# An encoder block on one core: x handed in with channels on partitions, values projected in chunks of the depth

## The chip, the core and the metric

The kernel runs on one core of a Trainium2 chip. The metric is the device time of one execution in microseconds. Six engines take part: TensorE (PE; its weight loads are PEld), VectorE (DVE), ScalarE (ACT), GpSimd (POOL), and SyncE (SP), which issues most of the transfers; ScalarE and GpSimd have DMA queues of their own.

## The reference

One layer of a hybrid encoder, over two requests of 512 and 256 tokens (768 rows of 2048 channels, float32) with shared weights:

```python
h = rmsnorm(x, ln_mix_g)
z = h @ w_in                                  # 2048 x 2560: fourier 1024 | q 1024 | k 256 | v 256
of = fourier_mix(zf, w_fourier)               # Re(2-D DFT over positions and group channels), then a map per group
oa = window_attention(rope(q), rope(k), v, sink)   # 16 q heads, 4 kv heads of 64, window +-128
mixed = concat([rmsnorm(of, g_f), rmsnorm(oa, g_a)])
x = x + mixed @ w_out
u = relu(rmsnorm(x, ln_mlp_g) @ w_up)         # 2048 -> 8192
x = x + (u * u) @ w_down
y = rmsnorm(x, ln_final_g)
```

`rmsnorm` divides each row by the root of its mean square (plus 1e-6) and multiplies the channels by a gain.

## The kernel before

Every matrix product is made of three passes of a rounded 32-bit format: each operand is split into a high part (a rounding copy on ScalarE) and a low part (what is left, a subtraction on VectorE), and high x high, high x low and low x high are summed in PSUM. The function `split` (L66) does this.

The stages follow each other on TensorE. In the first, rows of x (`xt`, six blocks of 128) are transposed on TensorE (`four`, L435), multiplied by the gains of the channels while they leave PSUM (`evacuate`, L443) into `xr`, split into `xs` or into spare places, and multiplied with the 256 value columns of w_in (`v_proj`, L378), one row block after the other. ScalarE squares each row block as a whole (`row_norm`, L374); the factor `r0` per row is put on the values when they are split, and on all partitions as `rb` by a small matmul (`row_scale`, L398). Two of the split parts are also stored to DRAM as b11h and b11l (L508).

The second stage, `product7` (L256), forms the 1024 Fourier columns from 28 products of 24 passes: a scheme with seven products in place of eight over halves of the depth and of the tokens. Around product n the loop at the end of the second `with` block forms sums of weights (`sum7`), the high part of the weights for product n + 3 (`high7`, ScalarE), the low part for n + 2 (`low7`, VectorE), the operands of later products (`xsum`, `xhigh`, `xlow`), issues the loads for n + 5 (`load7`, on SP) and takes finished products out (`out7`). Near the end b11h and b11l are read back (`first_block`, L322).

The third stage projects q and k (the loop with `piece_load` and `piece_split`, L765 and L773) while the Fourier transform of the groups runs beside it; `fold(g)` there multiplies by `rb`. Its weights' columns are permuted while they are split. Attention and the output projection follow (`trans`, L900, turns the probabilities into th and tl), then the MLP.

In the first two stages the order on SP, ScalarE and VectorE is the order of the program text; a queue or an engine that waits holds everything that stands behind the waiting instruction.

## Time and profile before

| | us |
|---|---|
| median of 3 runs | 2588.84 (2587.99 to 2588.94) |
| span of the profiled execution | 2587.1 |
| TensorE busy | 2575.2 (100%) |
| VectorE busy | 1814.0 (70%) |
| ScalarE busy | 1124.0 (43%) |
| GpSimd busy | 250.6 (10%) |

The profiled execution took 2587.1 us from its first to its last instruction; the timed runs stand 1.7 us above that. By line, two lines of the MLP (L1195 and L1630) have 71% of the chain that ended last, the first three stages together about a tenth. The sections of the profile used below are the waits of TensorE, the chain of waits, the timeline, groups of instructions by line and shape, windows of time and the DMA issues.

### The profile page before, as it was taken

The page shows a single profiled execution, that of the slowest core. Times are in us where ns is not written, and L with a number is a line of the kernel's source. Part 1 is how long each engine was busy: PE and PEld are TensorE (multiplying, and loading weights), DVE is VectorE, ACT ScalarE, POOL GpSimd, SP SyncE. Part 2 cuts the span into 40 slices and gives each one's busy share as a digit, 9 for nine tenths or more (in the row PEclk, how much of TensorE's full clock was granted, in tenths as well). Part 3 has the DMA queues.
Part 4 walks back from the last instruction along what each step waited for, and adds up shares of the span by engine and source line. Part 5 has one row for each costly group of instructions (what it writes and reads, how often), then busy time and mean ns, then how long its engine had stood idle before and what let it go on. Part 6 is the DMA issues. An engine that isn't in the chain of part 4 may idle for free.

```text
span 2587.1 us, 35019 instructions
## 1 busy us (share of the span) xinstructions
PE 2575.2 (100%) x13580; PEld 2359.9 (91%) x13580; DVE 1814.0 (70%) x2222; ACT 1124.0 (43%) x1574; POOL 250.6 (10%) x353
## 2 busy tenths in 40 slices
PE   9999999999999999999999999999999999999998
PEld 9999998888899999999999999988888888888887
DVE  7966568776555656555877877667776765777687
ACT  6545437674333333333444544433333333333335
POOL 1001422222201011000000000110000000000000
PEclk9999999999999999999999999999999999999999
DMA  7863467555664445456666666675543662555364
GB/s 258 311 221 112 135 222 220 147 151 194 222 193 159 163 160 188 159 190 236 214 215 232 231 212 208 247 303 176 185 154 110 219 232 82 179 179 165 98 207 155
DMA packets 281879, 494.27 MB, mean 191 GB/s; under 512 B 20288, under 2 KB 177008, under 8 KB 280432
## 3 DMA queue, kind: packets, MB, share of 16 engines
q1 hardware_dynamic: 210208, 325.98, 39.7%
q10 hardware_dynamic: 58688, 115.18, 11.8%
q0 software_dynamic: 12816, 50.87, 5.8%
q8 instruction: 107, 1.75, 0.3%
q14 instruction: 60, 0.49, 0.1%
HBM read 365.07 MB, written 126.88 MB: 190 GB/s over the span
## 4 chain that ended last, share of the span: by engine, by line
PE 96%; DVE 1%; DMA 1%; issue 1%; ACT 0%; POOL 0%; SPq 0%; POOLq 0%; DVEq 0%; ACTq 0%
PE pu L1195 36%; PE pd L1630 35%; PE pm L1048 10%; PE p L268 4%; PE pz L804 4%; PE pv L391 1%; PE o L926 1%; PE s L850 1%; PE t L907 1%; DMA ofr<-ofd 0%; PE ptx L137 0%; PE pe L631 0%; DMA zf<-zf 0%; PE pa L610 0%; PE pt L137 0%
## 5 line engine op out<-in xcount | busy, mean ns | idle before, releaser
L1195 PE MATMUL pu<-xf,wh 128*128 128x384 f32 x3072 | 781.0, 335 | 0.0
L1195 PEld LDWEIGHTS pu<-xf,wh 128*128 128x128 f32 x3072 | 554.2, 188 | 1.5 <-ACT o L1213 1.2
L1630 PE MATMUL pd<-wh,sh 128*128 128x512 f32 x1332 | 518.5, 389 | 0.0
L1630 PE MATMUL pd<-wl,sh 128*128 128x512 f32 x1332 | 518.4, 389 | 0.0
L1630 PE MATMUL pd<-wh,sl 128*128 128x512 f32 x1332 | 518.2, 389 | 0.0
L1195 PE MATMUL pu<-xf,wl 128*128 128x384 f32 x1536 | 513.9, 335 | 0.0
L1607 ACT ACTIVATE wh<-rd 128x1024 fp32r<-128x1024 f32 x200 | 202.4, 1054 | 521.9 <-PE pd L1630 422.2
L1617 DVE TENSOR_TENSOR wl<-rd,wh 128x1024 fp32r<-128x1024 f32 x200 | 236.2, 1221 | 225.8 <-ACT wh L1607 225.1
L1175 ACT ACTIVATE wh<-ur 128x1024 fp32r<-128x1024 f32 x160 | 170.0, 1063 | 382.7 <-PE pu L1195 211.3
L1630 PEld LDWEIGHTS pd<-wl,sh 128*128 128x128 f32 x1332 | 250.2, 188 | 51.7
L1630 PEld LDWEIGHTS pd<-wh,sl 128*128 128x128 f32 x1332 | 250.2, 188 | 51.7 <-DVE sl L1618 0.3
L1630 PEld LDWEIGHTS pd<-wh,sh 128*128 128x128 f32 x1332 | 250.2, 188 | 51.5
L1195 PEld LDWEIGHTS pu<-xf,wl 128*128 128x128 f32 x1536 | 288.5, 188 | 0.0
L1181 DVE TENSOR_TENSOR wl<-ur,wh 128x1024 fp32r<-128x1024 f32 x160 | 195.6, 1222 | 76.0 <-ACT wh L1175 76.0
L1216 DVE TENSOR_TENSOR o<-pu,o 128x768 f32<-128x768 f32 x160 | 152.9, 956 | 122.5 <-PE pu L1195 115.0
L1600 DVE TENSOR_TENSOR rd<-rd 128x1024 f32<-128x1024 f32 x112 | 131.8, 1218 | 0.0
L1195 PE MATMUL pu<-xs,wh 128*128 128x384 f32 x512 | 130.0, 334 | 0.0
L1175 ACT ACTIVATE wh<-sx 128x1024 fp32r<-128x1024 f32 x64 | 67.8, 1062 | 130.3 <-PE pu L1195 101.9
L268 PE MATMUL p<-xs,wh 128*128 128x384 f32 x448 | 114.0, 335 | 0.0
L1618 DVE TENSOR_TENSOR sl<-sr,sh 128x768 fp32r<-128x768 f32 x111 | 105.6, 951 | 0.0
L1181 DVE TENSOR_TENSOR wl<-sx,wh 128x1024 fp32r<-128x1024 f32 x64 | 78.2, 1223 | 23.8 <-ACT wh L1175 23.6
L1195 PEld LDWEIGHTS pu<-xs,wh 128*128 128x128 f32 x512 | 92.5, 188 | 0.0
(277 smaller groups left out, 3903.1 us busy)
## 6 DMA issues: line engine op xcount, KB each, us to landing
rd<-in_w_down SPq DMA_DIRECT2D x176, 512.0 KB, 5.1
ur<-in_w_up SPq DMA_DIRECT2D x128, 512.0 KB, 3.9
sr<-sd SPq DMA_DIRECT2D x95, 384.0 KB, 5.3
pd<-o ACTq DMA_DIRECT2D x60, 384.0 KB, 2.3
o<-pd POOLq DMA_DIRECT2D x60, 384.0 KB, 6.1
sd<-sm ACTq DMA_DIRECT2D x60, 384.0 KB, 2.9
raw<-in_w_in SPq DMA_DIRECT2D x38, 512.0 KB, 4.9
raw<-in_w_out SPq DMA_DIRECT2D x32, 512.0 KB, 4.9
```

The lines of the kernel that those rows point to most:

```text
L268: nc.tensor.matmul(ps7[bank, g, r][:, :HALF], l[:, i, r * P : (r + 1) * P], x[:, o, 4 * e + i, :], start=(opens and e == 0 and i == 0 and ...
L804: nc.tensor.matmul(ps[c][s][:, :HALF], w[:, i, cs], whole[j // 2][s][o][:, 4 * (j % 2) + i, :], start=first and n == 0, stop=stop and n == 2,)
L1048: nc.tensor.matmul(ps, l(k), w[:, k % 2, :], start=(k == 0 and n == 0), stop=(k == 7 and n == 2))
L1175: nc.scalar.activation(wh[:], raw[:], AF.Copy)
L1181: nc.vector.tensor_tensor(out=wl[:], in0=raw[:], in1=f32(wh[:]), op=ALU.subtract)
L1195: nc.tensor.matmul(ps[:, t, :HALF], w[:, i, t * P : (t + 1) * P], xb[:, o, i, :], start=(s == first_of[bank] and i == 0 and n == 0), stop= ...
L1216: nc.vector.tensor_tensor(out=o, in0=src, in1=o, op=ALU.add)
L1600: add = lambda x, y, op: nc.vector.tensor_tensor(out=x[:], in0=x[:], in1=y[:], op=op)
L1607: nc.scalar.activation(wh[:], t[:], AF.Copy)
L1617: nc.vector.tensor_tensor(out=wl[:], in0=t[:], in1=f32(wh[:]), op=ALU.subtract)
L1618: nc.vector.tensor_tensor(out=sl[:], in0=sr[:], in1=f32(sh[:]), op=ALU.subtract)
L1630: nc.tensor.matmul(o, l[:, q, ts], w[:, ns], start=(j == j0 and (q, t) == (0, 0)), stop=(j == j1 and (q, t) == (1, 2)),)
```

## The change

The host now hands x in a second time with channels on partitions (`x_t`), the three gains side by side, and w_in in blocks of 256 columns whose rows of one partition lie together; the q and k columns come in the order in which they are used. The values of all six row blocks are summed side by side in six PSUM banks, over nine chunks of the depth. The rows of x are loaded for their squares alone, during products 11 to 23, and the row factor `r0` is no longer put on the values but on the transposed probabilities in the attention; `rb` is made by a store to DRAM and a load to all partitions. The core of the diff (the functions that go away are in the listing above):

```diff
-    w_in = a["w_in"].rearrange("(k p) c -> p k c", p=P)
+    w_in = a["w_in"]
...
+    ssq = stat("ssq", NM * 4)
+    r0_d = dpool.tile([1, T], F32, tag="r0d", name="r0d")
...
-                    nc.sync.dma_start(raw[:], w_in[:, k0 : k0 + 4, c0 : c0 + 256])
+                    nc.sync.dma_start(raw[:], w_in[c0 // 256][:, k0 : k0 + 4, :])
...
+            flat = xs[1][:].rearrange("p o k t -> p (o k t)").rearrange("p (s o t) -> p s o t", s=8, o=2)
+            vt = xp.tile([P, 4, 2, HALF], F32R, tag="vt", name="vt")
+            room = [flat[:, 0:4], flat[:, 4:8], vt[:]]
+            chunks = [(0, 1), (1, 1), (2, 2), (4, 2), (6, 2), (8, 2), (10, 2), (12, 2), (14, 2)]
+            homes = [(0, 0), (0, 1), (0, 2), (1, 0), (1, 2), (2, 0), (0, 0), (1, 0), (2, 0)]
...
+            def load_x(k0, n):
+                for t in range(2):
+                    nc.sync.dma_start(xr[k0 // 8][t][:, k0 % 8 : k0 % 8 + n, :], a["x_t"][:, t, k0 : k0 + n, :])
+
+            def load_wv(k0, n, queue=nc.sync):
+                queue.dma_start(wv[k0 // 4][:, k0 % 4 : k0 % 4 + n, :], w_in[9][:, k0 : k0 + n, :])
+
+            def prepare(c):
...
+                for i in range(n):
+                    nc.scalar.activation(raw[0][:, i], raw[0][:, i], AF.Copy, scale=g0[:, k0 + i : k0 + i + 1])
+                gb = g0[:, k0 : k0 + n].rearrange("p (k o) -> p k o", o=1).to_broadcast([P, n, HALF])
+                nc.vector.tensor_tensor(out=raw[1], in0=raw[1], in1=gb, op=ALU.mult)
+                split(wh, wl, wv[w][:, wk, :])
+                for t in range(2):
+                    split(*parts[t], raw[t])
...
+            def v_term(c, m, term, i):
+                k0, n = chunks[c]
+                l, r = ((0, 0), (0, 1), (1, 0))[term]
+                k = k0 + i
+                nc.tensor.matmul(
+                    pv[m][:, :256], xhl[c][m // 3][l][:, i, m % 3 * P : (m % 3 + 1) * P], whl[k // 4][r][:, k % 4, :],
+                    start=(k == 0 and term == 0), stop=(k == NK - 1 and term == 2),
+                )
+
+            def v_keep(m):
+                split(vhl[:, m, :, 0, :], vhl[:, m, :, 1, :], pv[m][:, :256].rearrange("p (g d) -> p g d", g=NKV))
...
+            for i in range(15):
+                nc.tensor.matmul(pw[:, :P], ones[:], ones[:], start=True, stop=True)
+            nc.scalar.activation(mhalf[:, 7:8], mhalf[:, 7:8], AF.Copy)
+            nc.scalar.dma_start(gall[:], a["gains"])
+            load_wv(0, 1, nc.scalar)
+            load_x(*chunks[0])
+            load_wv(1, 1, nc.scalar)
+            load_x(*chunks[1])
...
+            for c, (k0, n) in enumerate(chunks):
+                prepare(c)
+                if c == 5:
+                    for o in range(2):
+                        nc.scalar.dma_start(b11_d[o][:], f32(xs[0][:, o]))
+                    nc.scalar.dma_start(ident[:], a["c_ident"])
+                if c + 1 < len(chunks):
+                    for term in range(3):
+                        for m in range(NM):
+                            for i in range(n):
+                                v_term(c, m, term, i)
                 else:
...
+                    for n2 in range(2):
+                        high7(n2)
+                        low7(n2)
+                    for m in range(NM):
+                        for term in range(3):
+                            for i in range(n):
+                                v_term(c, m, term, i)
+            for n in range(2):
+                xsum(b11, b12, b11, n)
+            for m in range(NM):
+                v_keep(m)
+
+        def row_load(i):
+            m, h = divmod(i, 4)
+            xt = raw7["x", i] = hq["p"].tile([P, 512], F32, tag="xt", name="xt", bufs=3)
+            nc.sync.dma_start(xt[:], x_rows(m)[:, h * 512 : (h + 1) * 512])
+
+        def row_square(i):
+            xt = raw7.pop(("x", i))
+            nc.scalar.activation(xt[:], xt[:], AF.Square, accum_out=ssq[:, i : i + 1])
+
+        def row_norms():
+            nc.vector.tensor_reduce(out=ss0[:], in_=ssq[:].rearrange("p (m h) -> p m h", h=4), op=ALU.add, axis=AX.X)
+            rsqrt_of(r0[:], ss0[:], D, NM, nc.gpsimd)
+            nc.gpsimd.dma_start(r0_d[0].rearrange("(m p) -> p m", p=P), r0[:])
+            nc.gpsimd.dma_start(rb[:], r0_d[0].partition_broadcast(P))
...
                 load7(n + 5)
+                for i in range(2 * n - 22, 2 * n - 20):
+                    if 0 <= i < 4 * NM:
+                        row_load(i)
+                    if 1 <= i <= 4 * NM:
+                        row_square(i - 1)
+                if n == 24:
+                    row_norms()
...
-                wh, wl = in_w[p] = [wpool.tile([P, 4, 256], F32R, tag=f"w{c}", name=f"w{c}", bufs=4) for c in "hl"]
-                hi, lo = (w[:].rearrange("p i (d h) -> p i h d", h=4) for w in (wh, wl))
-                split(hi, lo, raw[:].rearrange("p i (h d) -> p i h d", h=4))
+                in_w[p] = wsplit(raw)
...
-        later(t_th, lambda: nc.scalar.activation(th[:], pt[:], AF.Copy))
-        later(t_tl, lambda: nc.vector.tensor_tensor(out=tl[:], in0=pt[:], in1=f32(th[:]), op=ALU.subtract))
+        rk = r0[:, k0 + kb : k0 + kb + 1]
+        later(t_th, lambda: nc.scalar.activation(th[:], pt[:], AF.Copy, scale=rk))
+        later(t_tl, lambda: nc.vector.scalar_tensor_tensor(
+            out=tl[:], in0=pt[:], scalar=rk, in1=f32(th[:]), op0=ALU.mult, op1=ALU.subtract
+        ))
...
+    x = np.concatenate([given["x_prompt"], given["x_sample"]], 0)
+    given["x_t"] = x.T.reshape(NK, P, 2, HALF).transpose(1, 2, 0, 3)
+    given["gains"] = np.concatenate([given.pop(n) for n in _GAINS]).reshape(3 * NK, P).T
+    w = given["w_in"].reshape(NK, P, IN_W // 256, 256).transpose(2, 1, 0, 3)
+    turned = w[4:9].reshape(5, P, NK, 4, HD).swapaxes(3, 4).reshape(5, P, NK, 256)
+    given["w_in"] = np.concatenate([w[:4], turned, w[9:]], 0)
```

Three places of the order. First TensorE at the start. Before (pw are warm-up passes, pt and pg transposes, pv values; xs_290 and xs_291 hold the low or high parts of x's two halves):

```order
L474 MATMUL pw<-ones 128x128 x7
L137 MATMUL pt<-ident,xt_307 128x128 x4
L423 MATMUL pg<-ident,gt 128x16
L137 MATMUL pt<-ident,xt_307 128x128 x12
L474 MATMUL pw<-ones 128x128 x6
L391 MATMUL pv<-wh,xs_290 128x256 x16
L391 MATMUL pv<-wh,xs_291 128x256 x16
L137 MATMUL pt<-ident,xt_316 128x128 x8
L391 MATMUL pv<-wl,xs_290 128x256 x8
L137 MATMUL pt<-ident,xt_316 128x128 x8
L391 MATMUL pv<-wl,xs_291 128x256 x8
```

After:

```order
L417 MATMUL pw<-ones 128x128 x15
L407 MATMUL pv<-wh,xs_292 128x256 x3
L407 MATMUL pv<-wh,xs_293 128x256 x3
L407 MATMUL pv<-wl,xs_292 128x256 x3
L407 MATMUL pv<-wl,xs_293 128x256 x3
L407 MATMUL pv<-wh,xs_292 128x256 x3
L407 MATMUL pv<-wh,xs_293 128x256 x3
L407 MATMUL pv<-wh,xs_292 128x256 x3
L407 MATMUL pv<-wh,xs_293 128x256 x3
```

The transposes are gone from between the value passes, and each group of value passes now belongs to one slice of the depth and three row blocks.

Second, ScalarE in the same stage, around the two stores. Before:

```order
L462 ACTIVATE xs_291<-xr_287 128x512 x2
L462 ACTIVATE xs_291<-xr_289 128x512 x2
L72 ACTIVATE vhl<-pv,r_268 128x4x64
L375 ACTIVATE xt_531,ss_267<-xt_531 128x2048
L508 DMA b11h<-xs_290 128x3072
L508 DMA b11l<-xs_290 128x3072
L406 COPY rb<-pb 128x128
L462 ACTIVATE vt<-xr_287 128x512 x2
L462 ACTIVATE xs_291<-xr_289 128x512 x2
```

After, with what each waits for (DMAHW5 is the semaphore lane that the store b11h counts up; vt and xs_293 are places of split parts):

```order
L69 ACTIVATE wh<-raw 128x512 [waits DMAHW7_49]
L69 ACTIVATE vt<-xr_290 128x2x384 [waits Activation_49]
L69 ACTIVATE vt<-xr_291 128x2x384 [waits DVE_49]
L441 DMA b11h<-xs_292 128x3072
L441 DMA b11l<-xs_292 128x3072 [waits DMAHW2_49]
L442 DMA ident<-in_c_ident 128x128 [waits DMAHW5_49]
L394 ACTIVATE xr_290<-xr_290,gall 128x384 x2
L69 ACTIVATE wh<-raw 128x512
L69 ACTIVATE xs_293<-xr_290 128x2x384 [waits PE_49,Activation_49]
L69 ACTIVATE xs_293<-xr_291 128x2x384 [waits DVE_49,PE_49]
```

The identity load, which stood first of all before, now stands behind the stores with a wait for the lane of the first one, and the scaling and splitting of the next chunk stand behind it.

Third, SP near the end of `product7`. Before (wr are weights of a product, xf the parts read back, raw on L79 the weights of the next stage):

```order
L225 DMA wr<-in_w_in 128x4x256 x2
L79 DMA raw<-in_w_in 128x4x256
L225 DMA wr<-in_w_in 128x4x256
L326 DMA xf_1761<-b11h 128x3072
L79 DMA raw<-in_w_in 128x4x256
L326 DMA xf_1762<-b11l 128x3072
L225 DMA wr<-in_w_in 128x4x256
L79 DMA raw<-in_w_in 128x4x256 x4
```

After, with waits (xt are the row loads, of which each waits for a square on ScalarE):

```order
L227 DMA wr<-in_w_in 128x1024 [waits DMAHW1_49,DVE_49]
L79 DMA raw<-in_w_in 128x1024 [waits DMAHW5_49,DMAHW2_49,DVE_49]
L464 DMA xt<-in_x_sample 128x512 [waits DMAHW3_49,Activation_49]
L464 DMA xt<-in_x_sample 128x512 [waits DMAHW4_49,Activation_49]
L328 DMA xf_1647<-b11h 128x3072 [waits DMAHW5_49]
L328 DMA xf_1648<-b11l 128x3072 [waits DMAHW0_49,DVE_49]
L227 DMA wr<-in_w_in 128x1024 [waits DMAHW1_49]
L464 DMA xt<-in_x_sample 128x512 [waits DMAHW2_49,Activation_49]
L464 DMA xt<-in_x_sample 128x512 [waits DMAHW3_49,Activation_49]
L79 DMA raw<-in_w_in 128x1024 [waits DMAHW6_49,DMAHW2_49,DVE_49]
```

The last weight load of the stage now has row loads ahead of it as well as the two reads, and the last two row loads stand behind it.

## Rows read from the trace of the kernel before

**Rows 1.** Page, its head and part 1: busy us, share of the span, instructions.

```profile
span 2587.1 us, 35019 instructions
...
PE 2575.2 (100%) x13580; PEld 2359.9 (91%) x13580; DVE 1814.0 (70%) x2222; ACT 1124.0 (43%) x1574; POOL 250.6 (10%) x353
```

**Rows 2.** Waits of TensorE: total us, times, longest us.

```profile
PE pv L391 <- ACT wh L69: 1.1, 1, 1.1
...
PE pc L567 <- ACT of L633: 0.4, 1, 0.4
```

**Rows 3.** Chain of waits, 0 to 120 us: start us, us, what.

```profile
0.73 3.34 DMA ident<-in_c_ident
...
21.25 5.75 PE pv L391 x48
27.00 1.75 PE pt L137 x16
...
56.38 63.79 PE p L268 x368
```

**Rows 4.** Timeline of the start: start us, us, engine, line, instruction.

```profile
1.04 3.36 PE L474 MATMUL pw<-ones 128*128 128x128 f32 x14 [1.04 <-DVE mhalf L56]
...
1.65 1.28 ACT L462 ACT_TABLE_LOAD   x1 [1.65 <-PEq L1796]
...
7.96 1.50 PE L474 MATMUL pw<-ones 128*128 128x128 f32 x12
```

**Rows 5.** Groups of ScalarE, 0 to 57 us: busy us, mean ns, idle before.

```profile
L462 ACT ACTIVATE xs<-xr 128x512 fp32r<-128x512 f32 x20 | 12.2, 632 | 12.3 <-DVE xr L452 12.0 <-ACT xs L462 0.3
...
L69 ACT ACTIVATE wh<-raw 128x1024 fp32r<-128x1024 f32 x4 | 4.1, 1052 | 0.4 <-DMA raw<-in_w_in 0.3
L72 ACT ACTIVATE vhl<-pv,r 128x256 fp32r<-128x256 f32 x7 | 3.2, 462 | 1.9 <-PE pv L391 1.9
```

**Rows 6.** Timeline of VectorE, two low parts of product weights.

```profile
91.58 1.22 DVE L253 TENSOR_TENSOR wl<-wr,wh 128x1024 fp32r<-128x1024 f32 x1
...
140.54 1.23 DVE L253 TENSOR_TENSOR wl<-wr,wh 128x1024 fp32r<-128x1024 f32 x1 [0.44 <-ACT wh L245]
```

**Rows 7.** Windows of 1 us: busy us by engine, PEclk, DMA share, GB/s.

```profile
1.00:2.00 1.00, 0.96 (x4) 0.96 (x5) 0.00 (x1) 0.35 (x1) 0.00 (x0) 1.00 0.14 23
8.00:9.00 1.00, 1.00 (x12) 1.00 (x11) 1.00 (x3) 0.69 (x2) 0.00 (x0) 1.00 1.07 378
43.00:44.00 1.00, 1.00 (x12) 1.00 (x10) 1.00 (x2) 0.04 (x1) 0.74 (x2) 1.00 1.12 479
```

**Rows 8.** Timeline of ScalarE and its queue around the first store.

```profile
40.26 0.36 ACTq L508 DMA_DIRECT2D b11h<-xs  x1
...
40.69 0.45 ACT L72 ACTIVATE vhl<-pv,r 128x256 fp32r<-128x256 f32 x1
```

**Rows 9.** DMA issues, 56 to 176 us: count, KB each, median us to landing.

```profile
wr<-in_w_in SPq DMA_DIRECT2D x18, 512.0 KB, 6.8
...
xf<-b11h SPq DMA_DIRECT2D x1, 1536.0 KB, 9.2
```

**Rows 10.** Groups of ScalarE, 330 to 700 us.

```profile
L910 ACT ACTIVATE th<-t 128x512 fp32r<-128x512 f32 x56 | 32.7, 594 | 10.5 <-PE t L907 3.2 <-PE s L850 1.9 <-DVE tl L911 1.6
...
L1080 ACT ACTIVATE xc<-pm,r 128x512 f32<-128x512 f32 x24 | 16.3, 681 | 2.0 <-PE pm L1048 1.7
...
L1386 ACT ACTIVATE pm<-yp 128x512 f32<-128x512 f32 x14 | 8.4, 597 | 7.5 <-DVE yp L1380 7.3
...
L1386 ACT ACTIVATION_READ_ACCUMULATOR pm<-yp 128x1 f32 x14 | 2.6, 186 | 0.0
```

**Rows 11.** Window 104 to 152 us.

```profile
104.00:152.00 48.00, 48.00 (x279) 48.00 (x278) 39.88 (x34) 25.85 (x27) 0.00 (x0) 1.00 0.78 260
```

**Rows 12.** DMA issues, 0 to 60 us.

```profile
xt<-in_x_prompt SPq DMA_DIRECT2D x8, 256.0 KB, 5.9
```

**Rows 13.** Groups of ScalarE, 56 to 173 us.

```profile
L69 ACT ACTIVATE wh<-raw 128x1024 fp32r<-128x1024 f32 x4 | 8.2, 2051 | 6.3 <-PE p L268 3.8 <-DMA zf<-z 2.5
```

More of the change, by code (lines that the diff above doesn't have):

```diff
@@ new lines, in hybrid_encoder @@
+            whl = [[wpool.tile([P, 4, 256], F32R, tag=t, name=t, bufs=4) for t in ("wh", "wl")] for _ in range(4)]
+            flat = xs[1][:].rearrange("p o k t -> p (o k t)").rearrange("p (s o t) -> p s o t", s=8, o=2)
[3 more added lines that the diff above has]
+            homes = [(0, 0), (0, 1), (0, 2), (1, 0), (1, 2), (2, 0), (0, 0), (1, 0), (2, 0)]
@@ new lines, in hybrid_encoder @@
+            xhl = {}
+            def load_x(k0, n):
[5 more added lines that the diff above has]
+                k0, n = chunks[c]
+                r, s0 = homes[c]
+                ks = slice(k0 % 8, k0 % 8 + n)
+                raw = [xr[k0 // 8][t][:, ks, :] for t in range(2)]
+                rows = [room[r][:, s0 + i * n : s0 + i * n + n] for i in range(2 if k0 >= 8 else 1)]
+                if k0 < 8:
+                    parts = [[xs[0][:, o, ks, :] for o in range(2)]]
+                else:
+                    parts = []
+                parts += [[x[:, :, o, :] for o in range(2)] for x in rows]
+                xhl[c] = parts
+                w, wk = k0 // 4, slice(k0 % 4, k0 % 4 + n)
+                wh, wl = (x[:, wk, :] for x in whl[w])
+                for i in range(n):
[5 more added lines that the diff above has]
+                    split(*parts[t], raw[t])
@@ new lines, in hybrid_encoder @@
+            pv = [pp.tile([P, 512], F32, tag="f" if m < 4 else "ps", bufs=4, name="pv") for m in range(NM)]
+            def v_term(c, m, term, i):
+                k0, n = chunks[c]
+                l, r = ((0, 0), (0, 1), (1, 0))[term]
[4 more added lines that the diff above has]
+                )
@@ new lines, in hybrid_encoder @@
+            load_wv(1, 1, nc.scalar)
+            load_x(*chunks[1])
+            load_wv(2, 2)
+            load_x(*chunks[2])
+            load_wv(4, 4)
+            load_x(*chunks[3])
+            load_x(*chunks[4])
+            load_wv(8, 4)
+            load_x(*chunks[5])
+            load_x(*chunks[6])
+            load_wv(12, 4)
+            load_x(*chunks[7])
+            load_x(*chunks[8])
+            load7(0)
+            load7(1)
+            for c, (k0, n) in enumerate(chunks):
[9 more added lines that the diff above has]
+                                v_term(c, m, term, i)
+                else:
+                    for n2 in range(2):
[5 more added lines that the diff above has]
+                                v_term(c, m, term, i)
@@ L768, in piece_load @@
                 j, c0 = p % 4, cols[p // 4]
-                in_raw[p] = wload(w_in[:, 4 * j : 4 * j + 4, c0 : c0 + 256], 4, 256)
+                in_raw[p] = wload(w_in[c0 // 256][:, 4 * j : 4 * j + 4, :], 4, 256)
             elif p < n_in + 2:
```

146 lines of the change are left out of this document (9 added, 137 removed).

## Prediction

> **What bounds the kernel now.** I read the page first: TensorE is busy for 2575.2 of 2587.1 us [rows 1]. Its waits come next; the largest is 1.1, before the first value pass, and one of 0.4 in the z stage will matter below [rows 2]. So time can come only from work that TensorE no longer does or from an earlier start, and it can be lost to new gaps. The chain of waits of the first 120 us then says what TensorE does before `product7`: per block of 128 rows 48 value passes in 5.75 (0.12 each) and 16 transposes in 1.75, until the first product starts at 56.38; from there 368 passes follow without a gap, 0.1733 each, so a product (24 passes) is 4.16 [rows 3]. The run takes 2588.84 (median); the profiled one has a span of 2587.1. I leave the 1.7 around the span as it is and take the differences from 2588.84.
>
> **The start.** TensorE loses 96 transposes of x, the transposes of the gains and the row-scale passes. The 288 value passes stay, 288 x 0.12 = 34.6. They come in nine chunks of the depth, two of 18 passes (one slice) and seven of 36 (two slices, 36 x 0.12 = 4.32).
>
> When does the first one start? ScalarE begins with the table load (1.28 [rows 4]), from about 0.7 to 2.0, does a tiny activation until 2.2, issues the gains (0.44 for such an issue, an estimate from the issues beside it) and the first slice of w_v at 2.65. A small load, the identity, took 3.34 to land [rows 3]; so gains 5.5, w_v 6.0. Per slice ScalarE scales 384 columns, splits 256 and splits 384 twice. 256 columns took 0.46, 512 0.63, 1024 1.05 [rows 5]; I take 0.5 + 0.46 + 2 x 0.5 = 1.96 for one slice, 2 x 0.5 + 0.63 + 2 x 0.85 = 3.33 for two. The first pass has its operands at 5.5 + 0.5 + 0.46 + 0.5 = 7.0; ScalarE is through with chunk 0 at 7.5, with chunk 1 at 9.4, and has the first operand of chunk 2 at 9.4 + 1.0 + 0.63 + 0.85 = 11.9, the second 0.85 later, so TensorE gets into chunk 2 at about 12.2. From there TensorE's 4.32 a chunk is the longest: ScalarE needs 3.33, VectorE (a gain multiply and two low parts of 768 columns, one of 512, at 1.22 for 1024 [rows 6]) about 3.5. A chunk's transfers, 1.05 MB at the 378 GB/s seen while loads pile up [rows 7], take 2.8. Without a stall the values end at 12.2 + 7 x 4.32 = 42.4 and the first product starts 56.4 - 42.4 = **14.0 earlier**. The six splits of the values now lie together behind that point; product 0 has other PSUM banks, so they cost 0, and 6 x 0.46 = 2.8 if it had to wait for them all.
>
> **A new wait in that stage.** Behind chunk 5 ScalarE issues the stores b11h and b11l and then the identity load, which waits for b11h's completion; chunk 6's scaling is queued behind it. Before, b11h went out at 40.26 and the next activation ran at 40.69 [rows 8]: nothing was held. The issue is now at 9.4 + 4 x 3.33 = 22.8. The rate with both stores alone reached 479 GB/s [rows 7]; b11h's 1.57 MB at that are 3.3, with a little over 1 to start and end about 4.5. But SP still loads x and w_in then, and the same block on its way back took 9.2 among other loads [rows 9]. So the wait ends 4.5 to 11 after the issue (9.2 and a fifth more), at 27.3 to 33.8. Chunk 6 then needs 1.0 + 0.63 + 0.85 = 2.5 before its first pass, which TensorE wants at 12.2 + 4 x 4.32 = 29.5: a stall of 0.3 to 6.8. I take **3.1**, a landing of 7.3, between the ends, since SP's loads run out while the store is under way. The Trainium skill, DMA: Bandwidth & Descriptors, section Queues, rings and completion order, says that a DMA engine takes turns between the queues that have work for it, a packet at a time. By this rule b11h, with every second turn, would move for 6.6 instead of 3.3, land after 7.8, and the stall would be 3.6. No row of before has two loaded queues side by side long enough to test it, and the sum goes without it.
>
> **The row norms.** 24 loads of 256 KB and 24 squares (128x512 with an accumulator read) come into products 11 to 23. The nearest pair, L1386, is 0.60 + 0.19, overlapping by about 0.1 [rows 10]: 0.68, or 1.4 a product. ScalarE was busy 25.85 of 48 us there [rows 11], 2.2 a product; 3.6 of 4.16 fits. But ScalarE now also waits for loads, and the weights' high parts stand behind. There are three buffers and load i goes out when square i-3 is done, so two squares and two landings L must fit in three products: 2 (L + 0.75) < 12.5, L < 5.5. Loads of 512 KB landed here after a median of 6.8 [rows 9], those of 256 KB at the start after 5.9 [rows 12]. At 5.9 a product would take 4.43, 3.3 more over 12 products; at 6.8 it is 5.03, 10.4 more. The weights' low parts stood ready some 5 us ahead for product 10 (92.8, product at 98.0) and 10 for product 23 (141.8, product at 152.1) [rows 3, 6]; a mean cover of 7 takes that much off. Bounds 0 and 10.4; I take **+3.4** (6.8 with the cover), the more so as the last two squares stand in front of a weight's high part with two 1.5 MB reads before their loads on SP.
>
> **Smaller terms.** Columns turned beforehand take the 20 splits of the q/k weights from 2.05 [rows 13] to 1.05 [rows 5] on ScalarE, on VectorE alike. The 0.4 in the z stage goes [rows 2]: **-0.4**, with 0 as the other bound. In the attention 56 copies of 594 become like the 681 with a row scale [rows 10], 4.9 of ScalarE; VectorE's 56 subtractions become scaled ones, taken alike. TensorE's passes of L1048 hide both, since its list of waits has nothing of theirs [rows 2]: 0, and 9.8 if that cover were gone. The row scale goes to DRAM in 768 pieces of 4 bytes and back to all partitions; from product 24 there are four products, 16.6, for two landings: 0 while each is under 8, and 3 if one takes 11.
>
> **Sum:** 2588.84 - 14.0 + 3.1 + 3.4 - 0.4 = 2580.9, that is 7.9 faster; its own range is 2577.5 to 2584.5.
>
> **Rivals.** (a) Both stalls are hidden: the store lands in 4.5 and the row loads keep under 5.5. 2588.8 - 14.0 + 0.3 - 0.4 = 2574.7. For it: the cover of 5 to 10. Against: SP's traffic at both places.
> (b) The gain is eaten: the store takes 11 (+6.8), and L is 6.8 with only the cover of 5 (+5.4): -14.0 + 6.8 + 5.4 - 0.4 = -2.2, 2586.6, no change. For it: the 9.2 and the median of 6.8.
> (c) Slower: the row loads and the weights' loads starve each other. In 104 to 152 the queues moved 260 GB/s at a share of 0.78 [rows 11]; 6.3 MB more in 50 us is 126 GB/s, in all 386, as much as was moved while loads piled up [rows 7]. If L goes to 8.6, a product takes (8.6 + 0.75) x 2/3 = 6.23, 24.9 more over 12, 17.9 after a cover of 7: -14.0 + 3.1 + 17.9 - 0.4 = +6.6, 2595.4. It decides from L = 7.8 (5.7 a product), where nothing of the gain is left. Against it: w_in now comes in 4 KB runs instead of 1 KB, and the loads may shift by the cover.
> (d) TensorE starts on its low clock. The granted clock reads 1.00 (2.4 GHz) from the first microsecond [rows 7], but the first 14 warm-up passes took 0.24 each and 12 later ones 0.125 [rows 4], which is 1.2 against 2.4 GHz. Now 15 passes end at 4.6 and TensorE rests until 7.0, where before it went on with transposes. If the first 36 value passes took 0.24, they would end at 15.6, 3.4 late: 2584.3. The Trainium skill, TensorE: Matmul & The Clock Gate, Part 1, holds that the low clock is the default, that activity releases it and that rest brings it back; by that the rest speaks for (d), and rows of before show only the rise.
>
> **How the numbers follow.** Forecast 0.43, (a) 0.16, (b) 0.19, (c) 0.14, (d) 0.08. Under 0.2% (5.2 us) a measurement can't tell this kernel from unchanged. Faster: (a), 0.39 of the forecast, half of (d), 0.59. Slower: (c), 0.14. Within 0.2%: the rest, 0.27. To hold the time 8 times in 10 the range goes from (a) past (b), half way to (c): 2574.5 to 2591.
>
> **What would show it.** The first product starts at 45 to 46, with one gap of TensorE of about 3 before chunk 6 and ScalarE idle until the identity load goes out: the first two terms are right; without that gap, (a). Gaps of 3 to 4 in all between products 17 and 27, ended by a high or low part of a weight: the third. If from product 14 on most products take over 5 and ScalarE's idle ends with row loads, (c). Value passes of 0.24 at the start, (d). A new gap after 175 us would prove wrong what I cost at nothing there.

## The result, and the profile after

The changed kernel takes 2594.49 us (median of 9 runs, 2593.0 to 2597.2) beside 2588.88 for the kernel before on the same chip (9 runs): a ratio of 1.0024, 95% interval 1.0014 to 1.0033. It is 5.6 slower. The forecast was 2580.9 and the range ended at 2591.0; both missed.

The page's head and part 1 of the changed kernel, which answer to [rows 1]: TensorE works 4.3 less than before, and yet the span is 5.4 longer.

```profile
span 2592.5 us, 34872 instructions
...
PE 2570.9 (99%) x13474; PEld 2351.7 (91%) x13474; DVE 1791.3 (69%) x2204; ACT 1116.8 (43%) x1619; POOL 241.9 (9%) x339
```

The waits of TensorE over the whole of it (total us, times, longest), where [rows 2] had 1.1 and 0.4:

```profile
PE p L270 <- ACT wh L247: 4.3, 1, 4.3
PE pv L407 <- ACT xs L69: 4.1, 2, 3.6
PE p L270 <- DVE z L287: 1.2, 1, 1.2
...
PE p L270 <- DVE wl L255: 0.9, 2, 0.7
...
PE p L270 <- ACT z L290: 0.3, 1, 0.3
```

Two waits of about 4 are new: one in the values (L407), one in `product7` (L270). To see in which stage the time went I took the start of each stage's first TensorE pass from the timeline (the products on L270, the q and k projection, the scores, the up and the down projection) and subtracted, in one profiled execution of each kernel:

| | first product at | product stage | q/k stage | scores to first up pass | up | first down pass to the end of the last |
|---|---|---|---|---|---|---|
| before | 56.1 | 116.6 | 205.2 | 352.8 | 933.8 | 914.5 |
| after | 47.9 | 128.0 | 204.3 | 354.3 | 934.7 | 914.5 |

The start gave 8.2 instead of 14.0 less a stall of 3.1. The product stage took 11.4, that is these 8.2 and 3.2 more. Behind it the two differ by 1.5 in all up to TensorE's last pass, and by 0.7 in what follows that pass: 5.4 together, as in the spans.

**The start.** TensorE's timeline of the changed kernel (start us, us, engine, line, instruction, count, idle before):

```profile
1.04 6.33 PE L417 MATMUL pw<-ones 128*128 128x128 f32 x30 [1.04 <-DVE mhalf L56]
7.12 0.96 PE L407 MATMUL pv<-wh,xs 128*128 128x256 f32 x6
...
12.18 1.12 PE L407 MATMUL pv<-wh,xs 128*128 128x256 f32 x7 [0.49 <-ACT xs L69]
...
33.34 2.39 PE L407 MATMUL pv<-wh,xs 128*128 128x256 f32 x12 [3.62 <-ACT xs L69]
35.53 2.46 PE L407 MATMUL pv<-wl,xs 128*128 128x256 f32 x12
...
47.91 0.52 PE L270 MATMUL p<-xs,wh 128*128 128x384 f32 x2
```

The first value pass comes at 7.12 (forecast 7.0), chunk 2 at 12.18 (12.2); then TensorE rests 3.62 before chunk 6. The 15 warm-up matmuls are two passes each, 30 in all; the last of them starts at 7.09, so TensorE doesn't rest before the first value pass. ScalarE and its queue there, which answer to [rows 8]:

```profile
21.33 0.34 ACTq L441 DMA_DIRECT2D b11h<-xs  x1
...
30.54 0.34 ACTq L442 DMA_DIRECT2D ident<-in_c_ident  x1
30.92 1.12 ACT L394 ACTIVATE xr<-xr,gall 128x384 f32<-128x384 f32 x2 [8.76 <-DMA b11h<-xs]
```

The store landed after 9.19; the identity load waited for it, and chunk 6's scaling stood behind that load. After the rest comes something that the sum had no term for: the next 24 passes start 2.19 per 12 and then 2.30, against 1.44 per 12 elsewhere. Windows of the changed kernel (us, then busy us by engine, PEclk, DMA share, GB/s) show why:

```profile
34.00:38.00 4.00, 4.00 (x23) 4.00 (x22) 4.00 (x6) 4.00 (x9) 0.00 (x0) 0.57 0.59 233
...
164.00:170.00 6.00, 5.54 (x16) 5.03 (x17) 5.44 (x8) 3.80 (x6) 3.09 (x3) 0.50 0.46 165
```

The granted clock fell to its lower level (0.50 is 1.2 GHz) after each of the two long rests. The first cost about 1.6 (4.49 for 24 passes instead of 2.88), the second more: from 164.21 two products took 11.7 instead of 8.3.

**The product stage.** Of its 11.4, 6.7 are listed as TensorE's waits on L270. Taken from the starts of the passes, against the 0.1733 from one to the next in the kernel before, the whole can be placed: 4.4 in the long wait behind the pass at 159.6, 3.4 at the low clock behind it, and 3.7 in six short waits ahead of it (11.5; the stage before has 0.1 of such excess itself). The chain of waits there (start us, us, what):

```profile
151.28 11.13 DMA xt<-in_x_sample
...
163.46 0.71 ACT wh L247
```

SP's timeline says why these row loads were late and what stood behind others:

```profile
100.06 4.55 SPq L464 DMA_DIRECT2D xt<-in_x_prompt  x2
104.71 0.38 SPq L227 DMA_DIRECT2D wr<-in_w_in  x1
...
147.59 1.33 SPq L328 DMA_DIRECT2D xf<-b11h  x1
150.38 0.33 SPq L328 DMA_DIRECT2D xf<-b11l  x1
...
151.28 1.42 SPq L464 DMA_DIRECT2D xt<-in_x_sample  x2
```

At 100.06 SP stands 4.55 at row loads that have no free place among the three, and the weights' load waits behind them. From 48 to 176 us SP waits for squares 16 times, 22.0 in all:

```profile
SPq L464 <- ACT xt L468: 22.0, 16, 3.7
```

At 151.28 the last two row loads go out just behind the two reads of 1.5 MB. ScalarE's groups of the changed kernel (busy us, mean ns | idle before), the first from 48 to 176 us, the second from 330 to 700 us:

```profile
L468 ACT ACTIVATE xt<-xt 128x512 f32<-128x512 f32 x24 | 15.0, 626 | 21.2 <-DMA xt<-in_x_prompt 11.0 <-DMA xt<-in_x_sample 10.1
...
L69 ACT ACTIVATE wh<-raw 128x1024 fp32r<-128x1024 f32 x2 | 2.1, 1059 | 2.2 <-DVE z L287 1.1 <-DVE ss L471 1.1
```

```profile
L874 ACT ACTIVATE th<-t,r 128x512 fp32r<-128x512 f32 x56 | 37.9, 685 | 9.1 <-PE t L870 2.8 <-PE s L813 2.4 <-DVE tl L875 1.7
```

A square and its read are 0.63 and 0.19, as taken from [rows 10]; what was not foreseen is the 21.2 that ScalarE waits for rows, 8.6 of them for the last two loads. The q/k splits fell from 2051 ns [rows 13] to 1059, the probabilities' copies rose from 594 [rows 10] to 685, both as forecast. The DMA issues from 48 to 176 us (count, KB each, median us to landing) answer to [rows 9]:

```profile
wr<-in_w_in SPq DMA_DIRECT2D x21, 512.0 KB, 6.4
...
xt<-in_x_prompt SPq DMA_DIRECT2D x16, 256.0 KB, 5.5
...
xt<-in_x_sample SPq DMA_DIRECT2D x8, 256.0 KB, 5.6
...
r0d<-r POOLq DMA_DIRECT2D x1, 3.0 KB, 11.4
```

Loads did not get slower on the whole: weights 6.4 against 6.8 before, rows 5.5. From 104 to 152 us the queues moved 320 GB/s at a share of 0.91 against 260 and 0.78 [rows 11]:

```profile
104.00:152.00 48.00, 46.12 (x263) 44.99 (x262) 35.68 (x31) 35.84 (x65) 0.00 (x0) 1.00 0.91 320
```

### The profile page after: what moved, and what is told of

It reads as the page before. It is cut to its first block, busy times and chain, and to the rows that moved or that the text cites. A ratio compares the mean times of both kernels' runs of the same rounds, so it can differ in the third digit from the quotient of the medians.

```text
span 2592.5 us, 34872 instructions
## 1 busy us (share of the span) xinstructions
PE 2570.9 (99%) x13474; PEld 2351.7 (91%) x13474; DVE 1791.3 (69%) x2204; ACT 1116.8 (43%) x1619; POOL 241.9 (9%) x339
## 4 chain that ended last, share of the span: by engine, by line
PE 89%; DMA 5%; DVE 3%; ACT 1%; issue 1%; POOL 0%; SPq 0%; ACTq 0%; DVEq 0%; POOLq 0%
PE pu L1161 36%; PE pd L1596 35%; PE pm L1014 9%; PE pz L767 3%; PE p L270 1%; PE o L892 1%; PE s L813 1%; PE t L870 1%; DMA xt<-in_x_prompt 1%; DMA zf<-z 1%; PE pv L407 1%; DMA raw<-in_w_in 1%; POOL zy L652 0%; DMA ofr<-ofd 0%; DMA ql<-zs 0%
## 5 line engine op out<-in xcount | busy, mean ns | idle before, releaser
L1141 ACT ACTIVATE wh<-sx 128x1024 fp32r<-128x1024 f32 x64 | 67.8, 1061 | 131.4 <-PE pu L1161 100.0
L270 PE MATMUL p<-xs,wh 128*128 128x384 f32 x448 | 116.2, 340 | 5.8 <-ACT wh L247 4.3
```

The source lines that it names most:

```text
L270: nc.tensor.matmul(ps7[bank, g, r][:, :HALF], l[:, i, r * P : (r + 1) * P], x[:, o, 4 * e + i, :], start=(opens and e == 0 and i == 0 and ...
L1141: nc.scalar.activation(wh[:], raw[:], AF.Copy)
```

## The experiments

All stand on the changed kernel, except e9, which stands on the one before. The table has the same stages as above, with the median and the ratio to the kernel before on the same chip. The up projection lasts 933.8 to 935.2 in all of them but e10, the down projection 914.3 to 914.5. Stages come from one execution each and vary: the product stage, which e1, e7 and e8 leave alone, is 128.0 in the changed kernel and 128.7, 130.1 and 131.4 in these.

| | first product | product stage | q/k stage | scores to up | median us | ratio (interval) |
|---|---|---|---|---|---|---|
| e1 identity early | 41.8 | 128.7 | 203.8 | 353.7 | 2589.82 | 1.0002 (0.9992 to 1.0012) |
| e2 loads only | 48.5 | 125.5 | 213.9 | 354.3 | 2600.99 | 1.0048 (1.0033 to 1.0063) |
| e3 squares only | 47.4 | 117.5 | 205.6 | 354.4 | 2585.38 | 0.9989 (0.9979 to 0.9998) |
| e4 no row work | 48.0 | 116.6 | 204.2 | 354.8 | 2584.54 | 0.9985 (0.9976 to 0.9994) |
| e5 six places | 48.7 | 118.5 | 213.7 | 353.7 | 2592.25 | 1.0014 (1.0004 to 1.0023) |
| e6 reads later | 48.5 | 120.8 | 210.8 | 353.6 | 2594.87 | 1.0022 (1.0012 to 1.0032) |
| e7 filler | 46.0 | 130.1 | 203.9 | 353.6 | 2593.91 | 1.0019 (1.0009 to 1.0029) |
| e8 plain split | 48.5 | 131.4 | 203.8 | 354.1 | 2594.28 | 1.0023 (1.0012 to 1.0034) |
| e9 layout only | 55.8 | 116.6 | 203.7 | 352.6 | 2588.17 | 0.9997 (0.9987 to 1.0007) |
| c1 all three | 41.9 | 117.8 | 205.0 | 354.9 | 2577.35 | 0.9955 (0.9940 to 0.9970) |
| c2 c1, no store | 42.1 | 117.9 | 205.2 | 353.5 | 2577.72 | 0.9956 (0.9941 to 0.9971) |
| e10 e5, no store | 48.7 | 118.7 | 206.6 | 353.5 | 2596.46 | 1.0022 (1.0010 to 1.0034) |

**e1: the identity load goes out on SP, ahead of the weights' first loads.**

```diff
             load_x(*chunks[8])
+            nc.sync.dma_start(ident[:], a["c_ident"])
             load7(0)
...
-                    nc.scalar.dma_start(ident[:], a["c_ident"])
```

> The identity is loaded on SP behind the last load of x, not on ScalarE behind the store b11h; all else as in the change. In the changed kernel (2594.5) ScalarE waits 8.76 us there, TensorE 3.62, and its next 24 value passes take twice their time at a granted clock of 0.50; the first product starts at 47.9. Theory A (the two losses, at the identity and in the product stage, are separate and add): the first product starts at 42.4 to 42.8, the whole run takes 2589. Rival B (the product stage is bound by its loads, which don't come earlier): the first product starts as early, but the stage ends within 2 us of where it ended, 175.9, and the time is 2592.5 to 2594.5.

The first product starts at 41.8, 6.1 earlier; the time falls by 4.7 against the changed kernel (2594.49, on a chip where the kernel before took 0.5 less). So the wait and the low clock behind it cost what the stage says, and the product stage keeps its 128.7: the two losses are separate. The waits of e1:

```profile
PE p L270 <- ACT wh L247: 4.7, 1, 4.7
...
PE pv L407 <- ACT xs L69: 0.7, 2, 0.5
```

**e2 to e4: which part of the row work costs.** e2 keeps the 24 loads and has GpSimd read each tile in place of ScalarE's square; e3 loads one tile and squares it 24 times into a spare place; e4 drops both. So e2 and e4 leave the row norms out, and e3 has those of one tile.

```diff
-            nc.scalar.activation(xt[:], xt[:], AF.Square, accum_out=ssq[:, i : i + 1])
+            nc.gpsimd.tensor_scalar(   # e2
+                out=ssq[:, i : i + 1], in0=xt[:, :1], scalar1=0.0, scalar2=512.0, op0=ALU.mult, op1=ALU.add
+            )
...
-                        row_load(i)
+                        if i < 1:   # e3
+                            row_load(i)
+                        raw7["x", i] = raw7["x", 0]
...
-                for i in range(2 * n - 22, 2 * n - 20):   # e4: the loop goes
+            nc.vector.memset(ssq[:], 512.0)
```

> The 24 row loads stay where they are, but ScalarE does not square them: GpSimd reads one column of each, and the row norms are left out (every row's mean square is taken as 1). Theory A (ScalarE, waiting for row loads in its order, holds the high parts of the weights): the product stage falls from 128.0 to 118 or less and the time to 2585. Rival B (the 6.3 MB themselves delay the weights' loads): the stage stays at 126 or more, the time at 2593 to 2595. Rival C (ScalarE's time for the squares is too much): like A here, but unlike it in the run with squares and no loads.

> One row load, and 24 squares of that one tile in the places of the 24 squares; so ScalarE has their time but no wait for loads, and the row norms are not those of the rows. Theory A (waits for loads in ScalarE's order): the product stage at 118 or less, 2585. Rival B (bytes): 2584 to 2585 as well, since the bytes are gone. Rival C (ScalarE's 16 us of squares themselves): the stage stays above 122, the time above 2589.

> Neither row loads nor squares: the row norms are left out (every mean square is taken as 1), the rest of the change stays, with the wait at the identity. It gives the full price of the row work in the product stage. If the stage then takes 28 x 4.16 = 116.5, the time is 2594.5 - 11.5 = 2583. If something else in the change delays the weights (the earlier start of the products, with the same loads), the stage stays some us longer than 116.5 and the time above 2585.

e4 gives the whole price: 11.4 in the stage, 10 in time. e3 has the squares and nearly none of it (0.9), so ScalarE's own time is not the cost. e2 missed what the first theory expected: its product stage is 125.5, and its time is 6.5 above the changed kernel, because its q/k stage takes 213.9 with a wait for wf, the weights of the Fourier map:

```profile
PE pc L534 <- DMA wf<-in_w_fourier: 6.1, 1, 6.1
```

In its product stage the SP timeline shows another jam, of the same kind:

```profile
100.36 13.44 SPq L464 DMA_DIRECT2D xt<-in_x_prompt  x2
```

SP stood 13.44 until a place came free, with the weights behind: GpSimd's first three reads of a column took 8.59, where later ones take 0.2 to 0.4. So e2 doesn't measure the bytes, as I had meant it to; it shows that a load that waits for its place on SP holds the weights whoever frees the place.

**e5 and e6: uncouple the two.** e5 has six places and squares four loads behind (the places are cut from the diff); e6 reads b11h and b11l three steps later, behind the row loads.

```diff
-                    if 1 <= i <= 4 * NM:
-                        row_square(i - 1)
+                    if 4 <= i < 4 * NM + 4:              # e5, with six places in turn
+                        row_square(i - 4)
...
-        step(low_at, 22, first_block)
+        step(low_at, 25, first_block)                    # e6
```

> The change with six places for row loads in place of three (three more in the tile of the block difference, free by then), and each square four loads behind its load in place of one. Loads alone made the product stage 125.5 us long because SP stood 13.4 us at one row load waiting for a place, weights behind it. Theory A2 (SP waits for a place, ScalarE for a load, and the weights stand behind both): with six places the stage falls from 128.0 to 117 to 120, the time from 2594.5 to 2585 to 2587. Rival B (the queues' bytes): the loads land as late, the stage stays at 125 or more, 2592 or more.

> The reads of b11h and b11l (1.5 MB each) are put on SP behind the last weight load and the last row loads, three products later; all else as in the change, where the 23rd row load landed 11.1 us after its issue behind them and TensorE waited 4.27, then ran its passes at half speed for some 6 us. Theory A2, for the end of the stage: the wait of 4.27 and the 3.4 of slow passes go, the stage takes about 120.5, the time is 2587; the z stage may wait up to 2 us for the reads. Rival B: the bytes only come in another order, the stage stays at 126 or more.

With all 24 loads and all 24 squares e5's product stage is 118.5: 9.5 of the 11.4 are gone, as expected of the coupling, and for these bytes are ruled out. SP's waits for squares fall from 22.0 to this:

```profile
SPq L470 <- ACT xt L474: 6.9, 3, 4.3
```

e5 has two edits in one, so it doesn't tell what the places and what the later squares are worth by themselves. e6 takes 7.2 off: most of the price sits in the last two row loads behind the two reads. The 9.5 and the 7.2 overlap, since both take away the long wait and the low clock behind it. But the time did not follow: they lost 9.4 and 6.5 in the q/k stage, where e5 and e6 have these waits of TensorE (in e5 wf's load stands on SP behind loads of 512 KB, of which one landed after 12.0):

```profile
PE pc L538 <- DMA wf<-in_w_fourier: 6.8, 1, 6.8
```

```profile
PE pz L767 <- DVE z L287: 5.2, 1, 5.2
```

e5's windows there (GB/s is the last column), and GpSimd's timeline:

```profile
168.00:170.00 2.00, 2.00 (x14) 2.00 (x12) 0.27 (x1) 1.06 (x1) 0.00 (x0) 1.00 1.03 375
...
172.00:174.00 2.00, 2.00 (x12) 2.00 (x13) 0.00 (x0) 0.00 (x0) 0.00 (x0) 1.00 1.23 47
174.00:176.00 2.00, 2.00 (x13) 2.00 (x12) 0.00 (x0) 0.00 (x0) 0.00 (x0) 1.00 0.50 33
176.00:178.00 2.00, 2.00 (x14) 2.00 (x13) 0.00 (x0) 0.00 (x0) 0.00 (x0) 1.00 0.38 16
```

```profile
165.88 0.94 POOL L479 DMA_DIRECT2D r0d<-r  x1 [0.30 <-POOL r L101]
178.96 0.57 POOL L480 DMA_DIRECT2D rb<-r0d  x1 [12.14 <-DMA r0d<-r]
```

While the row factors go out in 768 pieces of 4 bytes, there are 6 us in which the DMA engines are busy and move next to nothing; the time goes into single packets of the weights' loads, which take up to 6.4 us. That made the store the next suspect; c2 and e10 take it away.

The store alone doesn't make the loss. The changed kernel has it beside the same stage (in flight from 169.4 to 180.7, stage from 175.9) and loses nothing there: 204.3. What differs is the order on SP. In the changed kernel, e1, e7 and e8 the first load of wf stands behind four loads of the q and k weights; in e2 to e6, c1, c2 and e10 it stands behind six, as in the kernel before, though no edit asked for that.

**e7: 14 matmuls of ones, of two passes each, stand in the wait before chunk 6.**

```diff
                 prepare(c)
+                if c == 6:
+                    for i in range(14):
+                        nc.tensor.matmul(pw[:, :P], ones[:], ones[:], start=True, stop=True)
```

> 14 passes pairs of ones into a scratch bank (3.5 us of TensorE) stand between chunk 5 and chunk 6, in the wait for the identity; all else as in the change. Theory D (the rest of 3.6 us costs twice: itself, and 24 passes at a granted clock of 0.50 behind it): the clock stays at 1.00, the first product starts at 46.1 to 46.3 in place of 47.9, the time falls by about 1.7. Rival (the slow passes have another cause, such as operands that come late): the first product stays at 47.9.

The operands of chunk 6 come 0.4 earlier (32.93), but its passes run at full rate, and the first product starts at 46.0, 1.9 earlier:

```profile
32.93 1.71 PE L407 MATMUL pv<-wh,xs 128*128 128x256 f32 x12 [1.15 <-ACT xs L69]
34.48 1.60 PE L407 MATMUL pv<-wl,xs 128*128 128x256 f32 x12
```

So the term "low clock after the rest" is real. In the time only 0.6 of it arrives, within the spread. e7's product stage is 2.1 longer than that of the changed kernel; as e8's, with nothing changed there, is 3.4 longer, it isn't shown that the earlier start was lost to that stage.

**e8: the probabilities' high part is copied without the row factor, and the low part subtracted without it.**

```diff
-        later(t_th, lambda: nc.scalar.activation(th[:], pt[:], AF.Copy, scale=rk))
+        later(t_th, lambda: nc.scalar.activation(th[:], pt[:], AF.Copy))
```

> The transposed probabilities are split without the row factor, as before the change; the values then lack the factor of their row norm, everything else is the change. From the first score pass to the first pass of the up projection the change takes 354.3 us, the kernel before 352.8. Theory: the scaled copy (681 in place of 594 ns) and the scaled subtraction lengthen ScalarE's and VectorE's way to a block's output, and this is where the 1.5 go: 352.5 to 353, and 1.5 less in all. Rival (the different arrival at the stage decides, not the scale): it stays at 354.

The copies fall back to 595 ns, and the stage from the first score to the first up pass stays at 354.1 against 354.3: TensorE's passes hide them, as the prediction had it. What the 1.5 are stays open; the stage lies between 352.6 and 354.9 in all executions here. The group in e8:

```profile
L873 ACT ACTIVATE th<-t 128x512 fp32r<-128x512 f32 x56 | 32.8, 595 | 11.3 <-PE t L870 2.7 <-PE s L813 2.5 <-DMA oad<-os 1.6
```

**e9: the kernel before, with w_in alone in blocks and its q and k columns turned by the host.**

```diff
-    w_in = a["w_in"].rearrange("(k p) c -> p k c", p=P)
+    w_in = a["w_in"]
...
-                    nc.sync.dma_start(raw[:], w_in[:, k0 : k0 + 4, c0 : c0 + 256])
+                    nc.sync.dma_start(raw[:], w_in[c0 // 256][:, k0 : k0 + 4, :])
```

> The kernel before the change with only the host's new layout of w_in: blocks of 256 columns (4 KB runs), q and k columns in order of use, plain splits for them; x, gains, value projection and row norms as before. Theory: the loads of w_in are hidden in that kernel and the splits too, but for 0.4 to 0.6 us in the z stage: 2588.4 (0 to -1.5). Rival (smaller runs had cost TensorE in the start, where the weights of the values are waited for): the first value pass comes 1 to 2 earlier, 2586 to 2587.

Neither the longer runs nor the shorter splits show in the time beyond the interval (0.9987 to 1.0007). In the stages the q/k part is 203.7 against 205.2. On the kernel before, then, the layout costs nothing, and a gain of 1 or 2 can't be told from none.

**c1: e1, e5 and the reads one step later (step 23, behind the last weight's load).**

> Three edits together: the identity on SP, six places for row loads with squares four loads behind, the reads of b11h and b11l behind the last weight load. Apart they gave: first product at 41.8 in place of 47.9; product stage 118.5 in place of 128.0; 120.8 in place of 128.0. But with the latter two the z stage grew from 204.3 to 213.7 and 210.8, each with a wait behind loads that were under way while the row scale went to DRAM in 768 pieces of 4 bytes (12.8 and 13.2 us to land). If that store is what fills the DMA engines (theory E), the z stage is long here too: 41.8 + 118.5 + 210 to 214, the time 2585 to 2588. Rival (the jam came from the reads and row loads meeting the next stage's loads): with the reads and loads earlier by 6 us the z stage is back at 205, the time 2579 to 2581.

2577.35 (4 runs): 12.1 faster than the kernel before on the same chip, and 17 faster than the change as it was. Theory E, which had put the jam into the q/k stage here too and the time at 2585 to 2588, missed: the stage is 205.0, as the rival had it. TensorE's two largest waits behind the warm-up, and ScalarE's longest from 56 to 170 us:

```profile
PE pm L1020 <- DVE wl L70: 0.8, 1, 0.8
PE pz L773 <- DVE z L287: 0.6, 1, 0.6
```

```profile
ACT wh L69 <- DMA zf<-z: 9.3, 1, 9.3
```

The store still takes 12.0 here, and a transfer of z to zf beside it, which landed after 16.0, holds ScalarE for 9.3. But the store goes out at 149.5 instead of 165.9, 10 before the q/k stage begins, and nobody on TensorE is waiting yet. In e3 and e4 it goes out at 151.8 and 151.0, some 13 before that stage, and they lose nothing there either.

**c2 and e10: the row factor reaches all partitions by six small matmuls in place of the store and the load back**, c2 on c1, e10 on e5.

```diff
-            nc.gpsimd.dma_start(r0_d[0].rearrange("(m p) -> p m", p=P), r0[:])
-            nc.gpsimd.dma_start(rb[:], r0_d[0].partition_broadcast(P))
...
+            if g == 0:
+                for m in range(NM):
+                    dg = fp.tile([P, P], F32, tag="dg", name="dg", bufs=6)
+                    nc.gpsimd.tensor_scalar(
+                        out=dg[:], in0=ident[:], scalar1=r0[:, m : m + 1], scalar2=1.0, op0=ALU.mult, op1=ALU.mult
+                    )
+                    pb = pp.tile([P, 512], F32, tag="f", bufs=4, name="pb")
+                    nc.tensor.matmul(pb[:, :P], ones[:], dg[:], start=True, stop=True)
+                    nc.scalar.copy(rb[:, m * P : (m + 1) * P], pb[:, :P])
```

> The three edits of the run before this one, and the row scale no longer goes through DRAM: as in the kernel before the change, GpSimd scales the identity by each block's row factors and TensorE spreads it with six small matmuls, here in front of the first fold. Theory E (the 768 pieces of 4 bytes jam the DMA engines for 10 to 13 us): no load at 160 to 185 takes over 7 us to land, the z stage is 204 to 206 (1.5 of it the new passes), the time 2577 to 2579, 11 faster than before the change. Rival: the loads there land as late as without it, and the two kernels take the same time within 1.5.

> The changed kernel with the six places and the squares four loads behind (as e5_deep), and the row factor brought to all partitions by six small matmuls at fold(0) in place of the store to DRAM in 768 pieces and the load back. In e5_deep the store was issued at 165.88, landed after 12.8, and the loads issued around it took 9 to 11; TensorE then waited 6.8 for a wf load in the z stage, which lasted 213.7 (from its start to the first score) against about 205 without a jam. Theory E, the store of 768 pieces holds up the loads beside it there: without it the z stage lasts 205 to 207, the first score starts at 373 to 375, and the time is 2584.5 to 2586.5 (e5_deep had 2592.3 beside a kernel before of 2589.0). Rival F, the loads are late because the last row loads and the two reads of 1.5 MB press on the z stage's first loads from before: the z stage lasts 211 to 214 and the time is 2590 to 2593.

c2 takes the same time as c1, within 0.4: where the store has slack, taking it away gives nothing, and c2 decides nothing about theory E. In e10 the q/k stage is 206.6 instead of e5's 213.7 and the wait for wf is gone, the stage that theory E named. Its windows at the place of e5's hole:

```profile
172.00:174.00 2.00, 2.00 (x12) 2.00 (x13) 0.88 (x1) 1.06 (x1) 0.00 (x0) 1.00 0.78 263
174.00:176.00 2.00, 2.00 (x13) 2.00 (x13) 0.35 (x1) 0.18 (x1) 0.06 (x1) 1.00 0.87 227
```

e10's order on SP is e5's, so the store (with the load back) made e5's loss there, given that order. The time of e10 missed all the same: 2596.46. Its first up pass starts at 727.5, 7.1 before e5's, but the up projection then lasts 945.0 instead of 934.3 with no wait of TensorE in it. Of its 12 runs three took 2585.1 to 2587.9, about what theory E had expected, and nine 2595.7 to 2601.9, the profiled one among them; that the other eight lost their time in the same place is not shown. What slowed the passes there stays open (the last section has the rows). Whether the store is also what cost e6 its 6.5 in the q/k stage was not tried; two weights' loads issued beside it landed after 13.3 there.

## Why the prediction was wrong

**Right.** Without a stall the first product starts 14.0 earlier: e1, without the identity's wait, starts it at 41.8 against the forecast 42.4. The starts at 7.0 and 12.2 came at 7.12 and 12.18. The row scale in the attention costs 0 (e8), the columns' order saves ScalarE's time and none that can be told in the whole (e9); from the q/k stage to the first up pass the change is +0.6 against the forecast -0.4, less than single executions differ by.

**Right by luck.** The 7.0 was put together from a w_v landing at 6.0 and ScalarE's first operands; ScalarE had the first operand at 6.62, and TensorE came at 7.12 because its warm-up passes went on until then. The prediction had counted 15 of them, an end at 4.6 and a rest until 7.0; they are 30, as 7 matmuls are 14 passes in [rows 4]. So the rest on which rival (d) stood never came, and that the values ran at full rate says nothing about what such a rest would do. The row scale's way through DRAM took 11.4 and then 7.4, over the 8 that "0 while each is under 8" had allowed, and still cost the changed kernel nothing; e5 paid for it.

**The identity's wait was +3.1 and cost 5.5.** The rest itself is 3.62, well inside 0.3 to 6.8: the issue came at 21.33 and not at 22.8, the landing took 9.19 and not 7.3, and the two nearly cancel, which is luck. The trace's packets say where the 9.19 went: for 2.9 after its issue nothing of the store moved, while SP's queue moved 408 GB/s; then the store's packets of 12 KB moved 318 GB/s beside 121 of SP's, in packets of 3 and 4 KB. The Trainium skill, DMA: Bandwidth & Descriptors, section Queues, rings and completion order, says that a DMA engine takes turns between queues with work, a packet at a time. The trace agrees in so far as the store, with the larger packets, moved more than SP's queue; the landing of 7.8 that I had worked out from the rule has no term for the 2.9 ahead of the first packet. What was missing is the price of the rest: 1.6 of passes at 1.2 GHz behind it (shown by e7). The Trainium skill, TensorE: Matmul & The Clock Gate, Part 1, says that rest brings the low clock back; the trace agrees, at 0.57 and 0.50 in the windows behind both long rests. Behind a rest of 3.0 in e7's product stage it read 0.50 too, behind the 1.2 in the changed kernel's 1.00. I had used that page for the start alone, where there was no rest, and had priced every stall at its own length.

**The step that failed: the row norms**, "Bounds 0 and 10.4; I take +3.4 (6.8 with the cover)". They cost 11.4 in the stage and 10 in time (e4). The sizes were not at fault: the median row load landed after 5.5 where the sum had 6.8, and a square took 0.61 from one to the next against 0.68. With 5.5 the prediction's own cycle is (5.5 + 0.75) x 2/3 = 4.17 a product against 4.16, which costs nothing. What failed is the model, a steady cycle that each product pays, less a mean cover of 7. It left out two things:
- The last two loads were named ("stand in front of a weight's high part with two 1.5 MB reads before their loads on SP") and not priced. They landed after 11.1 and 10.7 and made the 4.4 on TensorE, which brought the low clock with it, 3.4 more over two products: 7.8 of the 11.4. e6 moves the reads and takes 7.2 off the stage.
- The other 3.7 came in six short waits. SP and ScalarE stand in each other's way: SP waits in order for one of three places with weights' loads behind it (22.0), ScalarE waits in order for a row with a weight's high part behind it (21.2). With six places and later squares the waits ahead of the last loads come to 1.0 and what is left at the end to 1.1, at the same bytes (e5).

**The rivals.** Neither stall was hidden, as (a) wanted. The time fell nearest to (c), 2595.4, by luck. Its place was right, row loads against weights' loads, and its price came from the wrong mechanism: it wanted row loads of 8.6 for want of bandwidth, and they landed in 5.5 at 320 GB/s. Against it I had put that the loads "may shift by the cover"; loads that stand behind a waiting load on one queue can't shift. (b) had no change as the outcome, with the same two stalls at their upper ends: even those, +6.8 and +5.4, add to 4.7 less than what came, 5.5 and 11.4; the clock, which neither had in it, is 1.6 and 3.4 of that. The other places behaved: -14.0 + 5.5 + 11.4 and 1.5 for the stages behind make +4.4, against 4.7 between the two profiled executions' last passes; the 0.3 between them is the first product before, at 56.1 and not at the 56.4 that the sum had.

## What to carry to other kernels

Price a long stall on TensorE with the passes behind it at the low clock (the rests of 3.0, 3.6 and 4.3 had them here, the one of 1.2 had not), and price an in-order queue by what stands behind its waiting entry, not by bytes or a mean cover. A load that gets a new place in a shared queue needs places enough that it never waits there, and should not be put behind large reads whose data is not due. Count the warm-up passes in the trace and not in the program. When a repair frees one stage, look at what now falls due earlier in the next one: e5 and e6 gained 9.5 and 7.2 and lost most of it again, until the store of small pieces stood somewhere with slack (c1) or was gone (the q/k stage of e10). Read the order of the queues again in every experiment: an edit in one stage moved the first wf load behind two more loads in the next.

## What the runs showed of the hardware that was not expected

A store of 3 KB in 768 pieces of 4 bytes took 9.9 to 13.3 to land (e4 and e2 are the ends), and beside it in e5 the queues moved 16 to 47 GB/s for 6 us at shares of 0.38 to 1.23. In each of the ten kernels with the store, 2 to 13 DMA packets beside it took over 3 us, the longest 6.8 (e3); in the four without it (before, e9, c2, e10) none did in the first 250 us, the longest being 2.1. The trace lists the store as 16 packets of 192 bytes. That the pieces of 4 bytes are what holds the others up is not shown: only the whole way through DRAM was taken away.

In e10 the passes of the up projection became slower with the granted clock at 1.00 and no wait. Groups from 1000 to 1660 us, of e10 and then of e5 (busy us, mean ns):

```profile
L1174 PE MATMUL pu<-xf,wh 128*128 128x384 f32 x1986 | 512.0, 339 | 0.0
```

```profile
L1167 PE MATMUL pu<-xf,wh 128*128 128x384 f32 x2026 | 516.3, 336 | 0.0
```

It begins at 1087.3. Until then a pass starts 0.173 or 0.174 after the one before; there one comes after 0.275, and from it to the end of the projection every second pass takes 0.179. That is 0.1767 on the mean instead of 0.1733, or 1.9% for 585 us. In e5 and others the same steps appear for short stretches, worth 0.5 to 1.5 us. Nothing in the profile names a cause.
